# Layer-norm tiles turned back two steps behind, mixed features emitted in the next head, and four early output tiles stored, in a one-core mLSTM and HGRN2 step

## The chip, the cores and the metric

The kernel runs on one NeuronCore of one Trainium2 chip. The metric is the time of one execution on the device in microseconds. The core has a matrix engine (TensorE, PE in the profile, with its weight loads under PEld), a vector engine (VectorE, DVE), an activation engine (ScalarE, ACT), GpSimd (POOL), and SyncE (SP), which here only issues transfers. PE writes into PSUM; the kernel divides it into three pools of banks of 128 x 512 numbers: `mm` (three banks, projections and output tiles), `lv` (two) and `o` (three).

## What is computed

One layer of a decoder trunk over a prompt of 1024 tokens and eight samples of eight new tokens (64 rows, "tile 8" of nine 128-row tiles, in the kernel's words; the other eight tiles are the prompt). Everything is float32. The model width is 1024; four mLSTM heads with keys of 128 and values of 256, eight HGRN2 heads of 128.

```python
xn = rmsnorm(x, g_norm)
xm, zm, om, fh, qh, ih, zh = split(xn @ w_in)
xc = silu(causal_conv(xm)); q, k from xc, v from xm, per head; gates from [q, k, v]
# mLSTM, per chunk: C is the matrix memory, n its normaliser, m a running maximum
num = (q k^T * D) v + g * (q C);  den = rowsum(q k^T * D) + g * (q n)
h   = num / max(|den|, exp(-m));  C = decay * C + sum_s w_s k_s v_s^T
hm = layernorm(h, m_ln) * sigmoid(om)
hm = (hm + m_skip * xc) * silu(zm)             # the "mixed" features of the mLSTM heads
# HGRN2, per chunk: S = diag(f) S + k v^T, o = S^T q, k = 1 - f
oh = rmsnorm(o, h_norm) * silu(zh)
y = rmsnorm(x + concat(hm, oh) @ w_out, g_final)
```

The outputs are y for prompt and samples and the new states (conv rows, C, n, m and S).

## The kernel before

Float32 products are made of float32r parts: a number is split into a high and a low part, and `mm3` issues three matmuls (lines 94, 95, 96: high x high, low x high, high x low). The high part is a cast on ACT (for the input weights `whi`, line 147), the low part a subtraction on POOL (`wlo`, line 147) or DVE.

After a front (norms, conv, q, k, v of all mLSTM heads), the main part runs twelve heads in the order H0 M0 H1 M1 H2 M2 H3 M3 H4 H5 H6 H7, H an HGRN2 head (`hgrn_main`) and M an mLSTM head (`mlstm_main`). Each of these functions is a generator: it emits a piece of a head and yields a weight. `weave` takes that weight times a ratio and emits as many microseconds of side work between the pieces. The side work is the input projection of the heads to come, 48 pieces per head of weights times activations, and, at the end, the first output tiles (`early_out`). The order on PE is the order of this text (`tc.manual_schedule`); on the other engines and on the transfer queue the scheduler sets it, out of its own estimate of when each instruction is ready. A head's pieces all carry weights that sum to about `HEAD`, so that its 48 side pieces end with it.

An M head goes through eight prompt tiles j. Each is one step: PE makes the state update `pu`, the numerator `pn` (lines 94 to 96 on `o`), DVE folds C, and `layer_norm` makes the normalised tile `hn` (DVE line 657, with POOL and DVE small work ahead). `turn_back` transposes `hn` on PE (line 719) into an `lv` bank, and `onto_om` multiplies a pair of tiles onto the output gate `om` on DVE. Before, step j turns back tile j-1. Then the sample tile follows the same way (line 811), the eight sample states are updated on DVE (line 825), and last the mixed features are made for each half of the head: a load `xcr` of the conv output (line 835), `xcr * skip + om` on DVE (line 837), `* zm` on POOL (line 839), and a store to `mixd` in HBM (line 840).

An H head does its product over levels 1, 2, 4, ... 64 of the time axis. DVE makes Q and K (line 973, 937) for level 1, then `products(n)` folds gates and makes QK (lines 1005, 940, with `Sf` and `f` in 1008, 1010); PE multiplies them in groups (line 101), level 1 first, levels 2 to 8 as a group ("lower"), later 16 to 64 ("upper"). z is its gate path (line 880, on DVE from a projection in an `mm` bank).

At the end the output projection multiplies the 16 mixed features by `w_out`, in two halves of 512 columns. `wo_split` splits its weights, low halves alternately on DVE and POOL for the first half. `out_part(hf, t, g)` accumulates the first 15 features of tile t in an `mm` bank, `out_done` adds the 16th. The first five tiles (`EARLY`) are side work of the last H head; two of them are stored into `xr` (`out_store`, DVE line 1317) so that their banks are free, three stay in the three banks. Features of an output tile come back from HBM through `mraw`, with `mhi` and `mlo` on ACT and DVE (1266, 1267).

Of the kernel before, what the change touches and what calls it, by code (L numbers as in the profile page):

```python
# [30 lines left out]
def hybrid_step(  # L31
# [509 lines left out]
    def gate_scan():  # L541

        ig, y, lf, t1, m, b = [unit(s)[0:4, :T] for s in ("ig", "gy", "glf", "gt", "gm", "gb")]
        nc.sync.dma_start(out=gd, in_=GT)
        gv = gd.rearrange("(j r) t -> r j t", r=32)
        for g, dst in ((0, ig), (1, y)):
            nc.sync.dma_start(out=dst.rearrange("p (j t) -> p j t", t=272), in_=gv[4 * g:4 * g + 4])
            V.tensor_scalar(dst, dst, scalar1=bgt[:, g:g + 1], scalar2=None, op0=ALU.add)
        yield 1.0
        S.activation(t1, y, AF.Abs)  # L550
        S.activation(t1, t1, AF.Exp, scale=-1.0)
        S.activation(t1, t1, AF.Ln, bias=1.0)
        V.scalar_tensor_tensor(lf, y, 0.0, t1, op0=ALU.min, op1=ALU.subtract)
        lfs = lf[:, TP:T].rearrange("p (b c) -> p b c", c=8)[:, :, 0]
        igs = ig[:, TP:T].rearrange("p (b c) -> p b c", c=8)[:, :, 0]
        lm = small(8, "lm")
        V.tensor_tensor(lm[0:4, :], lfs, m0t, op=ALU.add)
        V.tensor_copy(t1, lf)
        V.memset(t1[:, TP:T].rearrange("p (b c) -> p b c", c=8)[:, :, 0], -1e30)
        V.tensor_copy(y, ig)  # L560
        V.tensor_tensor(y[:, TP:T].rearrange("p (b c) -> p b c", c=8)[:, :, 0], igs, lm[0:4, :], op=ALU.max)
        V.tensor_tensor_scan(m, t1, y, initial=0.0, op0=ALU.add, op1=ALU.max)
        yield 4.0
        G.memset(t1, 1.0)
# [12 lines left out]
        nc.sync.dma_start(out=o_sm[0].rearrange("b h -> h b"), in_=msl[0:4, :])
        yield 4.0
        ps = ps_o()
        for t in range(8):  # L580
            PE.transpose(ps[:, t * 8:t * 8 + 4], ig[:, t * P:t * P + P], ident[0:4, 0:4])
            PE.transpose(ps[:, t * 8 + 4:t * 8 + 8], m[:, t * P:t * P + P], ident[0:4, 0:4])
        for j in range(4):
            for o, src in ((64, ig), (68, m)):
                PE.matmul(ps[32 * j:32 * j + 32, o:o + 4], lhsT=src[:, TP + win(j):TP + win(j) + 32],
                          rhs=ident[0:4, 0:4], start=True, stop=True)
        V.tensor_copy(COLS.rearrange("p a b -> p (a b)"), ps[:, :72])
        S.activation(COLS[:, :, 4:8], COLS[:, :, 4:8], AF.Exp, scale=-2.0)
# [56 lines left out]
    def layer_norm(ps, t, h):  # L645
# [11 lines left out]
        V.tensor_scalar(hn, ps[:, 0:256], scalar1=mv[:, 0:1], scalar2=dd, op0=ALU.subtract, op1=ALU.mult)  # L657
        return hn

    def mlstm_main(h):  # L660
        d = ctxs.pop(("M", h))
        mln, msk = par("m_ln"), par("m_skip")
# [65 lines left out]
        yield 2.4  # L728
        tiles += pair_prep(1)
        yield 2.4  # L730
        C = tp = hn = None
        for j in range(8):
            Sv, kv, qv, vv = tiles[j]
            pu = ps_o()
# [11 lines left out]
            if j < 7:  # L746
# [1 line left out]
                Cs = (CC[:, o:o + VW], CC[:, o + VW:o + 2 * VW])  # L748
                S.copy(Cs[0], C)
                V.tensor_tensor(Cs[1], C, f32(Cs[0]), op=ALU.subtract)  # L750
            if j > 0:
                if j % 2:
                    tp = ps_lv()
                turn_back(hn, tp, (j - 1) % 2)
                if j % 2 == 0:
                    onto_om(tp, j // 2 - 1)
            hn = layer_norm(pn, j, h)
            if j % 2 and j < 5:
                tiles += pair_prep(j // 2 + 2)
                yield 2.4  # L760
            yield 2.8 if j else 4.2
        turn_back(hn, tp, 1)
        onto_om(tp, 3)
        nc.sync.dma_start(out=o_pC[0, 0, h], in_=C[:, 0:256])
        G.tensor_copy(NEW[:, h:h + 1], C[:, 256:257])

# [21 lines left out]
        for a in range(4):  # L788
# [5 lines left out]
        V.tensor_tensor(qm.rearrange("p (b c) -> p b c", c=72)[:, :, 0:8], q[:, TP:T].rearrange("p (b c) -> p b c", c=8),  # L794
                        Gt[:, TP:T].rearrange("p (b c) -> p b c", c=8), op=ALU.mult)
        yield 5.0
        pn = ps_o()
        for j in range(4):
            oj = pn[32 * j:32 * j + 32, :257]
# [5 lines left out]
                PE.matmul(oj, lhsT=qm[:, b * 64 + win(j):b * 64 + win(j) + 32], rhs=C0v[b // 4][:, b % 4, :],  # L805
                          start=False, stop=e == 1)
        hn = layer_norm(pn, 8, h)
        yield 3.0
        tp = ps_lv()
        for a in range(2):  # L810
            PE.transpose(tp[:, a * P:(a + 1) * P], hn[:, a * P:(a + 1) * P], ident)
        for a in range(2):
            oms, ts = compact(d["om"][a][:, TP:T]), spread(tp[:, a * P:(a + 1) * P])
            for e in range(2):
                V.scalar_tensor_tensor(oms[:, e], ts[:, e], mln[:, 2 * h + a:2 * h + a + 1], oms[:, e],
                                       op0=ALU.mult, op1=ALU.mult)
        for a in range(4):
            for g in range(2):
                pu = ps_o()
# [4 lines left out]
                cv = C0v[g][:, a, :]  # L824
                new = V.scalar_tensor_tensor(cv, cv, Gt[:, TP + 8 * b + 7:TP + 8 * b + 8], pu[:, :257],
                                             op0=ALU.mult, op1=ALU.add)
            yield 1.3
        NEWv = NEW[:, 4:36].rearrange("p (b h) -> p h b", h=4)
        for i in range(2):
            nc.sync.dma_start(out=o_sC[0, 4 * i:4 * i + 4, h].rearrange("b k v -> k b v"), in_=C0v[i][:, :, 0:256])  # L830
            G.tensor_copy(NEWv[:, h, 4 * i:4 * i + 4], C0v[i][:, :, 256])
        for a in range(2):
            ft = 2 * h + a
            xc = unit("xcr")
            nc.sync.dma_start(out=xc[:, :T], in_=xcd[ft])
            with tc.issue_after(getattr(new, "ins", new)):
                V.scalar_tensor_tensor(xc[:, :T], xc[:, :T], msk[:, ft:ft + 1], d["om"][a][:, :T],
                                       op0=ALU.mult, op1=ALU.add)
            G.tensor_tensor(xc[:, :T], xc[:, :T], d["zm"][a][:, :T], op=ALU.mult)
            nc.sync.dma_start(out=mixd[ft], in_=xc[:, :T])  # L840
            yield 1.8

    def norm_states():
        pt = ps_o()
# [72 lines left out]
    def hgrn_main(h):  # L917
# [316 lines left out]
    def wo_split(hf, i):  # L1234
        raw = wo_raw.pop((hf, i))
        if hf == 0 or i >= 6:
            hi, lo = XH[:, i * 1024:(i + 1) * 1024], XL[:, i * 1024:(i + 1) * 1024]
        else:
            hi, lo = unit("woh", F32R)[:, :1024], unit("wol", F32R)[:, :1024]
        S.copy(hi, raw)  # L1240
        (G if hf == 0 and i % 2 else V).tensor_tensor(lo, raw, f32(hi), op=ALU.subtract)
        for a in range(2):
            wo[(hf, 2 * i + a)] = (hi[:, a * 512:(a + 1) * 512], lo[:, a * 512:(a + 1) * 512])

# [35 lines left out]
    def out_part(hf, t, g):  # L1280
# [4 lines left out]
        ps = acc[(hf, t)]  # L1285
        mx = ctxs.pop("mix0") if (hf, t, g) == (0, 0, 0) else mix_prep(t, g)
        for k in range(len(mx)):
            stop = (hf, t, g, k) in ((0, 0, 1, 6), (0, 1, 1, 6))
            mm_out(ps, t, mx[k], wo[(hf, g * 8 + k)], g == 0 and k == 0, stop)
            if k % 2 or k + 1 == len(mx):  # L1290
                yield cost(6, 512)
# [6 lines left out]

    def out_store(t):

        if t == 0:
            part[1] = unit("xr")
        part[t] = part[1][:, t * HU:(t + 1) * HU]
        x_res(part[t], 0, t)
        V.tensor_tensor(part[t][:, :512], part[t][:, :512], acc.pop((0, t)), op=ALU.add)

# [42 lines left out]
            yield from g  # L1349

    STEPS = 48
    HEAD = {"H": 47.2, "M": 53.4}

    def weave(side, main, ratio):

# [14 lines left out]
                yield from islice(gates, 1)  # L1370
        yield from gates

    EARLY = 5

    def early_out():
        for t in range(EARLY):
            for g in range(2):
# [1 line left out]
                    for i in range(4 + 2 * g, 6 + 2 * g):  # L1379
                        wo_prep(0, i)  # L1380
                yield from out_part(0, t, g)
            if t < EARLY - 3:
                out_store(t)

    side = chain(*[(hgrn_in if kind == "H" else mlstm_in)(h) for kind, h in jobs], early_out())
# [18 lines left out]
    with tc.manual_schedule(engines={mybir.EngineType.PE}):  # L1404
        for i, (kind, h) in enumerate(jobs[:-1]):
            main = (hgrn_main if kind == "H" else mlstm_main)(h)
            extra = 0.0
            if i == 0:
                main, extra = with_gates(main, gates), 9.0
            weave(islice(side, STEPS), main, us / (HEAD[kind] + extra))  # L1410
        weave(side, hgrn_main(7), (us / 2 + EARLY * cost(45, 512)) / HEAD["H"])
        for t in range(9):
            out_done(0, t)
            if EARLY - 3 <= t < 6:
                run(chain(out_part(0, t + 3, 0), out_part(0, t + 3, 1)))
# [97 lines left out]
```

## Time and profile before

| | |
|---|---|
| median of 3 runs | 1219.85 us (1218.01 to 1223.15) |
| profiled execution | 1220.89 us, span of its instructions 1219.1 us |
| granted PE clock, mean | 0.983 |
| PE busy | 1139.4 us, 93% |
| DVE busy | 771.5 us, 63% |
| ACT busy | 437.4 us, 36% |
| POOL busy | 389.3 us, 32% |

A row of waits reads: engine, what waited, `<-` what released it, then the total in us, the times and the longest. A row of a timeline reads: start, length, engine, line, operation, output `<-` inputs, shape, how many in a row, and in brackets the engine's idle time just ahead with what ended it. A stretch reads: from, to, length, the engine's busy time with its instructions, the granted clock as a share of full speed, the share and the GB/s of the transfers.

### The profile page before, as it was taken

The page shows a single profiled execution, that of the slowest core. Times are in us where ns is not written, and L with a number is a line of the kernel's source. Part 1 is how long each engine was busy: PE and PEld are TensorE (multiplying, and loading weights), DVE is VectorE, ACT ScalarE, POOL GpSimd, SP SyncE. Part 2 cuts the span into 40 slices and gives each one's busy share as a digit, 9 for nine tenths or more (in the row PEclk, how much of TensorE's full clock was granted, in tenths as well). Part 3 has the DMA queues.
Part 4 walks back from the last instruction along what each step waited for, and adds up shares of the span by engine and source line. Part 5 has one row for each costly group of instructions (what it writes and reads, how often), then busy time and mean ns, then how long its engine had stood idle before and what let it go on. Part 6 is the DMA issues. An engine that isn't in the chain of part 4 may idle for free. (4 is left out here: it accounts for less than half of the span.)

```text
span 1219.1 us, 22869 instructions
## 1 busy us (share of the span) xinstructions
PE 1139.4 (93%) x9251; PEld 1064.6 (87%) x9251; DVE 771.5 (63%) x1474; ACT 437.4 (36%) x937; POOL 389.3 (32%) x508
## 2 busy tenths in 40 slices
PE   6899999979988999899998999899999989989997
PEld 5789999979988998899988998899999978767886
DVE  4674544595669466875669466876868686533443
ACT  5454444425321443134321453142424233333332
POOL 4443333223434343523434352533232331100000
PEclk9899999999999999999999999999999999989999
DMA  8133334123133232414132331412121245556652
GB/s 262 45 129 134 129 122 135 35 54 125 60 115 107 84 114 74 148 53 146 34 120 98 110 106 57 143 54 73 53 74 53 73 143 141 166 157 180 210 175 99
DMA packets 154061, 133.89 MB, mean 110 GB/s; under 512 B 11439, under 2 KB 130155, under 8 KB 153954
## 3 DMA queue, kind: packets, MB, share of 16 engines
q1 hardware_dynamic: 153954, 132.41, 34.6%
q8 instruction: 73, 1.20, 0.4%
q14 instruction: 34, 0.28, 0.1%
HBM read 93.96 MB, written 38.43 MB: 109 GB/s over the span
## 5 line engine op out<-in xcount | busy, mean ns | idle before, releaser
L94 PE MATMUL mm<-XH,whi 128*128 128x384 f32 (+1 forms) x1344 | 454.3, 338 | 0.9 <-DVE z L880 0.6
L95 PE MATMUL mm<-XL,whi 128*128 128x384 f32 (+1 forms) x1344 | 442.6, 329 | 0.0
L96 PE MATMUL mm<-XH,wlo 128*128 128x384 f32 (+1 forms) x1344 | 442.1, 329 | 0.0
L94 PEld LDWEIGHTS mm<-XH,whi 128*128 128x128 f32 x1344 | 255.7, 190 | 5.7 <-issue 1.7
L95 PEld LDWEIGHTS mm<-XL,whi 128*128 128x128 f32 x1344 | 255.9, 190 | 1.7 <-issue 1.3
L96 PEld LDWEIGHTS mm<-XH,wlo 128*128 128x128 f32 x1344 | 255.0, 190 | 0.0
L147 POOL TENSOR_TENSOR wlo<-wraw,whi 128x1024 fp32r<-128x1024 f32 x56 | 139.5, 2491 | 226.5 <-ACT whi L147 226.0
L147 ACT CAST whi<-wraw 128x1024 fp32r<-128x1024 f32 x56 | 58.9, 1051 | 123.4 <-PE mm L95 104.5
L94 PE MATMUL mm<-XH,mhi 128*128 128x512 f32 x144 | 59.2, 411 | 10.1 <-ACT lv L1322 4.6
L96 PE MATMUL mm<-XH,mlo 128*128 128x512 f32 x144 | 57.8, 401 | 1.2 <-DVE mlo L1267 1.2
L1266 ACT CAST mhi<-mraw 128x1024 fp32r<-128x1024 f32 (+1 forms) x32 | 31.9, 998 | 74.7 <-PE mm L95 56.2
L95 PE MATMUL mm<-XL,mhi 128*128 128x512 f32 x144 | 57.7, 401 | 0.0
L1335 POOL TENSOR_TENSOR rs<-rs,mhalf 128x1 f32<-128x1 f32 (+1 forms) x9 | 4.9, 542 | 158.3 <-DVE rs L1334 158.3
L1267 DVE TENSOR_TENSOR mlo<-mraw,mhi 128x1024 fp32r<-128x1024 f32 (+1 forms) x32 | 39.0, 1221 | 24.0 <-ACT mhi L1266 23.8
L940 DVE TENSOR_TENSOR QK<-hk,Sf 128x256 f32<-128x256 f32 x96 | 49.4, 555 | 0.0
L457 DVE TENSOR_TENSOR xml<-mm,xmh 128x384 fp32r<-128x384 f32 (+1 forms) x24 | 12.1, 508 | 52.2 <-ACT XB L456 45.0
L872 DVE TENSOR_SCALAR f<-f,OML,LB 128x384 f32<-128x384 f32 (+1 forms) x24 | 26.8, 1116 | 27.2 <-ACT f L870 27.1
L94 PEld LDWEIGHTS mm<-XH,mhi 128*128 128x128 f32 x144 | 27.9, 194 | 17.2 <-issue 5.0
L1008 DVE TENSOR_TENSOR Sf<-Sf,f 128x512 f32<-128x512 f32 (+1 forms) x48 | 40.1, 836 | 0.1
L892 ACT COPY iT<-mm 128x128 f32<-128x128 f32 x64 | 13.0, 270 | 73.3 <-PE mm L96 70.3
L473 DVE SCALAR_TENSOR_TENSOR Y<-XB,PAR,Y 128x1112 f32<-128x1112 f32 x24 | 38.1, 1589 | 0.2
L96 PE MATMUL mm<-woh,mlo 128*128 128x512 f32 x96 | 37.5, 391 | 0.3 <-DVE mlo L1267 0.3
(350 smaller groups left out, 2237.0 us busy)
## 6 DMA issues: line engine op xcount, KB each, us to landing
wraw<-in_w_in SPq DMA_DIRECT2D x56, 512.0 KB, 4.2
woraw<-in_w_out SPq DMA_DIRECT2D x16, 512.0 KB, 4.4
mraw<-mixd SPq DMA_DIRECT2D x16, 512.0 KB, 6.2
mraw<-mixd SPq DMA_DIRECT2D x16, 448.0 KB, 4.5
xcd<-XB SPq DMA_DIRECT2D x8, 544.0 KB, 2.7
qkd<-qk SPq DMA_DIRECT2D x16, 272.0 KB, 5.0
xcr<-xcd SPq DMA_DIRECT2D x8, 544.0 KB
mixd<-xcr SPq DMA_DIRECT2D x8, 544.0 KB
```

The source lines that it names most:

```text
L94: PE.matmul(out, lhsT=lh, rhs=rh, start=first, stop=False)
L95: PE.matmul(out, lhsT=lh, rhs=rl, start=False, stop=False)
L96: PE.matmul(out, lhsT=ll, rhs=rh, start=False, stop=last)
L147: return S.copy(hi, raw), G.tensor_tensor(lo, raw, f32(hi), op=ALU.subtract)
L457: V.tensor_tensor(ml[:, t0:t0 + m], ps[:, :m], f32(mh[:, t0:t0 + m]), op=ALU.subtract)
L473: V.scalar_tensor_tensor(Y[:, :1112], XB[:, j:j + 1112], cw[:, 8 * j + ft:8 * j + ft + 1], Y[:, :1112], op0=ALU.mult, op1=ALU.add)
L872: V.tensor_scalar(f[:, s], f[:, s], scalar1=OML[:, h:h + 1], scalar2=LB[:, h:h + 1], op0=ALU.mult, op1=ALU.add)
L892: S.copy(dst, ps[:, u * P:(u + 1) * P])
L940: i = V.tensor_tensor(dst, ksrc, ssrc, op=ALU.mult)
L1008: V.tensor_tensor(hv(Sf, W, n)[:, :, 0, :], hv(Sf, W, n)[:, :, 0, :], hv(f, W, n)[:, :, 1, n - 1:n].to_broadcast([P, ng, n]), op=ALU.mult)
L1266: S.copy(hi[:, :w * n], raw[:, :w * n])
L1267: V.tensor_tensor(lo[:, :w * n], raw[:, :w * n], f32(hi[:, :w * n]), op=ALU.subtract)
```

## The change

There are five parts.

1. `gate_scan`, woven into the first H head, yields 5.5 in place of 4.0, twice, and that head's weight grows from 9 to 12 on top.
2. The turn-back in an M head goes two steps behind (`hns` holds the tiles waiting), the last tile's after the 5.0 yield, the sample tile's in the second of the four state updates. Weights are changed (4.2 to 2.8, 3.0 to 2.0, 1.3 to 1.5, `HEAD["M"]` from 53.4 to 48.2).
3. The mixed features are put off (`deferred`) into the H head that follows, behind `products(2)` and `products(4)`; that head's weight grows by 3.6.
4. `wo_split` makes all low halves on DVE.
5. Four of the five early tiles are stored (`STORED`), two to a unit; out_part runs in the out_done loop from t = 3 to 6, for tile t+2, in place of t = 2 to 5, tile t+3.

```diff
-        yield 4.0
+        yield 5.5          # gate_scan, twice
...
+            if j > 1:
+                if j % 2 == 0:
+                    tp = ps_lv()
+                turn_back(hns.pop(0), tp, j % 2)
                 if j % 2:
-                    tp = ps_lv()
-                turn_back(hn, tp, (j - 1) % 2)
-                if j % 2 == 0:
                     onto_om(tp, j // 2 - 1)
-            hn = layer_norm(pn, j, h)
+            hns.append(layer_norm(pn, j, h))
...
-            yield 2.8 if j else 4.2
-        turn_back(hn, tp, 1)
-        onto_om(tp, 3)
+            yield 2.8
+        tp = ps_lv()
+        turn_back(hns.pop(0), tp, 0)
...
         yield 5.0
+        turn_back(hns.pop(0), tp, 1)
+        onto_om(tp, 3)
...
         hn = layer_norm(pn, 8, h)
-        yield 3.0
-        tp = ps_lv()
-        ...                # tile 8: transposes and products onto om
+        yield 2.0
         for a in range(4):
             ...            # two state updates
-            yield 1.3
+            if a == 1:
+                ...        # tile 8: transposes and products onto om
+            yield 1.5
...
-        for a in range(2):
+        def mixed(a):
             ft = 2 * h + a
             xc = unit("xcr")
             nc.sync.dma_start(out=xc[:, :T], in_=xcd[ft])
-            with tc.issue_after(getattr(new, "ins", new)):
-                V.scalar_tensor_tensor(...)
+            V.scalar_tensor_tensor(...)
             G.tensor_tensor(xc[:, :T], xc[:, :T], d["zm"][a][:, :T], op=ALU.mult)
             nc.sync.dma_start(out=mixd[ft], in_=xc[:, :T])
-            yield 1.8
+        deferred.extend([lambda: mixed(0), lambda: mixed(1)])
...
+        late = [deferred.pop(0) for _ in range(len(deferred))]      # hgrn_main
...
         for n in (2, 4, 8):
             lower.append(products(n))
+            if late:
+                with tc.issue_after(getattr(lower[-1][3], "ins", lower[-1][3])):
+                    late.pop(0)()
+                yield 1.8
             yield 3.3
...
-        (G if hf == 0 and i % 2 else V).tensor_tensor(lo, raw, f32(hi), op=ALU.subtract)
+        V.tensor_tensor(lo, raw, f32(hi), op=ALU.subtract)
...
-            stop = (hf, t, g, k) in ((0, 0, 1, 6), (0, 1, 1, 6))
+            stop = hf == 0 and t < STORED and (g, k) == (1, 6)
...
-    HEAD = {"H": 47.2, "M": 53.4}
+    HEAD = {"H": 47.2, "M": 48.2}
...
-    EARLY = 5
+    EARLY, STORED = 5, 4
...
-            if t < EARLY - 3:
+            if t < STORED:
                 out_store(t)
...
+            if kind == "H" and i and jobs[i - 1][0] == "M":
+                extra = 3.6
             if i == 0:
-                main, extra = with_gates(main, gates), 9.0
+                main, extra = with_gates(main, gates), 12.0
...
-            if EARLY - 3 <= t < 6:
-                run(chain(out_part(0, t + 3, 0), out_part(0, t + 3, 1)))
+            if 3 <= t < 7:
+                run(chain(out_part(0, t + 2, 0), out_part(0, t + 2, 1)))
```

PE issues the same 6141 rows in both. Line numbers of the changed kernel are a few higher (719 is 721 there, 837 is 843, 839 is 845, 940 is 947, 1005 is 1013, 1318 is 1330).

On PE, in the third M head (M2), the end of the step of tile 7: the numerator `o_...` of tile 7 is made, then a turn-back of `hn_...` into `lv_...`, then side work on `mm`. Before, the turn-back is of tile 6:

```order
L94 MATMUL o_6752<-vhl_6540,skl_6554 128x258
L95 MATMUL o_6752<-vhl_6540,skl_6554 128x258
L96 MATMUL o_6752<-vhl_6540,skl_6554 128x258
L94 MATMUL o_6752<-CC_6254,qgl_6544 128x258
L95 MATMUL o_6752<-CC_6254,qgl_6544 128x258
L96 MATMUL o_6752<-CC_6254,qgl_6544 128x258
L719 MATMUL lv_6761<-CF,hn_6727 128x128 x2
L94 MATMUL mm_6729<-XH,whi_6435 128x384
```

Now:

```order
L94 MATMUL o_6758<-vhl_6543,skl_6557 128x258
L95 MATMUL o_6758<-vhl_6543,skl_6557 128x258
L96 MATMUL o_6758<-vhl_6543,skl_6557 128x258
L94 MATMUL o_6758<-CC_6262,qgl_6547 128x258
L95 MATMUL o_6758<-CC_6262,qgl_6547 128x258
L96 MATMUL o_6758<-CC_6262,qgl_6547 128x258
L721 MATMUL lv_6724<-CF,hn_6684 128x128 x2
L94 MATMUL mm_6782<-XH,whi_6432 128x320
```

In its place now stands the turn-back of tile 5 (`hn_6684`); tile 6 is turned after the loop, eighteen side products later, and twelve side products and nine products of a tile lie between one turn-back and the next at this place.

On DVE, from the last sample state of the last M head into the H head behind it (M3 to H4). `xcr` is the mixed features, `hq` the last two q blocks, Q and K what PE needs for level 1. Before:

```order
L825 SCALAR_TENSOR_TENSOR C_1175_8339<-C_1175_8339,RB_7750,o_8514 128x257
L837 SCALAR_TENSOR_TENSOR xcr_8529<-xcr_8529,PAR,om_7353 128x1088
L880 TENSOR_TENSOR hq_8172<-hq_8172,mm_8467 128x384
L837 SCALAR_TENSOR_TENSOR xcr_8546<-xcr_8546,PAR,om_7580 128x1088
L880 TENSOR_TENSOR hq_8172<-hq_8172,mm_8518 128x320
L973 TENSOR_TENSOR Q_1209_8564<-hq_8172,f_8170 128x544
L937 COPY K_1210_8567<-hk_8171 128x256
L937 COPY K_1210_8567<-hk_8171 128x4x64
L988 COPY Sf_8563<-f_8170 128x544
L990 TENSOR_TENSOR f_8170<-f_8170 128x544
```

Now, in the same H head, the stretch behind the level-2 products, `QK_8655`, up to the level-4 products, `QK_8701`:

```order
L947 TENSOR_TENSOR QK_8655<-hk_8167,Sf_8553 128x4x32x2
L949 TENSOR_TENSOR QK_8655<-hk_8167,Sf_8553 128x64
L843 SCALAR_TENSOR_TENSOR xcr_8662<-xcr_8662,PAR,om_7347 128x1088
L971 COPY_PREDICATED A_1205_8551<-mk_364,lv_8606 128x288
L1016 TENSOR_TENSOR Sf_8553<-Sf_8553,f_8166 128x272x2
L974 COPY_PREDICATED A_1205_8551<-mk_365,lv_8606 128x144
L1018 TENSOR_TENSOR f_8166<-f_8166 128x272x2
L947 TENSOR_TENSOR QK_8701<-hk_8167,Sf_8553 128x64x4
L947 TENSOR_TENSOR QK_8701<-hk_8167,Sf_8553 128x4x16x4
L949 TENSOR_TENSOR QK_8701<-hk_8167,Sf_8553 128x64
L1013 TENSOR_TENSOR QK_8701<-hq_8168,f_8166 128x544
L1016 TENSOR_TENSOR Sf_8553<-Sf_8553,f_8166 128x136x4
```

The first `xcr` row has moved from ahead of Q and K to behind the level-2 products; the second stands two rows further down, ahead of the level-8 products. On PE, 90 side products now lie between the level-1 group and the lower group there, before 78; between the last sample-state product and the level-1 group there are 36, before 54.

On SP at the same place, the loads and stores (`wraw` a block of input weights, `out<-C` the sample states). Before:

```order
L140 DMA wraw_8722<-in_w_in 128x8x128
L835 DMA xcr_8529<-xcd 128x1088
L835 DMA xcr_8546<-xcd 128x1088
L830 DMA out<-C_1174_8338 128x4x256
L830 DMA out<-C_1175_8339 128x4x256
L840 DMA mixd<-xcr_8529 128x1088
L840 DMA mixd<-xcr_8546 128x1088
L140 DMA wraw_8904<-in_w_in 128x8x128
```

Now:

```order
L836 DMA out<-C_1174_8346 128x4x256
L836 DMA out<-C_1175_8347 128x4x256
L140 DMA wraw_8898<-in_w_in 128x8x128
L842 DMA xcr_8662<-xcd 128x1088
L842 DMA xcr_8708<-xcd 128x1088
L846 DMA mixd<-xcr_8662 128x1088
```

The `xcr` loads stood ahead of the state stores; now they stand behind them and behind the next weight load.

On DVE, at the output tiles, from the last rows of the last H head (z, `zl`, `zh`) to the adds onto `xr`. `wol` is a low half of the second half's output weights, `mlo` that of an output tile's features. Before:

```order
L1216 SCALAR_TENSOR_TENSOR z_10391<-lv_11661,PAR,z_10391 128x32 x2
L1146 TENSOR_TENSOR zl_11448<-z_10391,zh_11447 128x512
L1241 TENSOR_TENSOR wol_11780<-woraw_11777,woh_11779 128x1024
L1146 TENSOR_TENSOR zh_11447<-z_10391,zh_11447 128x64
L1318 TENSOR_TENSOR xr_11207<-xr_11207,o_11682 128x512
L1267 TENSOR_TENSOR mlo_11753<-mraw_11750,mhi_11752 128x896
L1318 TENSOR_TENSOR xr_11207<-xr_11207,o_11696 128x512
L1318 TENSOR_TENSOR xr_11710<-xr_11710,mm_11314 128x512
```

Now:

```order
L1253 TENSOR_TENSOR wol_11726<-woraw_11723,woh_11725 128x1024
L1279 TENSOR_TENSOR mlo_11741<-mraw_11738,mhi_11740 128x1024
L1228 SCALAR_TENSOR_TENSOR z_10391<-lv_11666,PAR,z_10391 128x32 x2
L1158 TENSOR_TENSOR zl_11448<-z_10391,zh_11447 128x512
L1158 TENSOR_TENSOR zh_11447<-z_10391,zh_11447 128x64
L1330 TENSOR_TENSOR xr_11207<-xr_11207,o_11687 128x512
L1279 TENSOR_TENSOR mlo_11771<-mraw_11768,mhi_11770 128x896
L1330 TENSOR_TENSOR xr_11207<-xr_11207,o_11701 128x512
L1330 TENSOR_TENSOR xr_11478<-xr_11478,o_11715 128x512
L1330 TENSOR_TENSOR xr_11478<-xr_11478,o_11729 128x512
```

The `wol` row has moved ahead of z and the first `mlo` of the next output tile; of the adds, the first four read `o` banks now, before two, and the third read an `mm` bank.

More of the change, by code (lines that the diff above doesn't have):

```diff
@@ L577, in gate_scan @@
         nc.sync.dma_start(out=o_sm[0].rearrange("b h -> h b"), in_=msl[0:4, :])
-        yield 4.0
+        yield 5.5
         ps = ps_o()
@@ L658, in layer_norm @@
         return hn
+    deferred = []
     def mlstm_main(h):
@@ L730, in mlstm_main @@
         yield 2.4
-        C = tp = hn = None
+        C = tp = None
+        hns = []
         for j in range(8):
@@ L750, in mlstm_main @@
                 V.tensor_tensor(Cs[1], C, f32(Cs[0]), op=ALU.subtract)
-            if j > 0:
+            if j > 1:
+                if j % 2 == 0:
+                    tp = ps_lv()
+                turn_back(hns.pop(0), tp, j % 2)
                 if j % 2:
-                    tp = ps_lv()
-                turn_back(hn, tp, (j - 1) % 2)
-                if j % 2 == 0:
                     onto_om(tp, j // 2 - 1)
-            hn = layer_norm(pn, j, h)
+            hns.append(layer_norm(pn, j, h))
             if j % 2 and j < 5:
@@ L807, in mlstm_main @@
         hn = layer_norm(pn, 8, h)
-        yield 3.0
-        tp = ps_lv()
-        for a in range(2):
[L811 to L816, printed above, removed]
+        yield 2.0
         for a in range(4):
@@ L826, in mlstm_main @@
                                              op0=ALU.mult, op1=ALU.add)
-            yield 1.3
+            if a == 1:
+                tp = ps_lv()
+                for b in range(2):
+                    PE.transpose(tp[:, b * P:(b + 1) * P], hn[:, b * P:(b + 1) * P], ident)
+                for b in range(2):
+                    oms, ts = compact(d["om"][b][:, TP:T]), spread(tp[:, b * P:(b + 1) * P])
+                    for e in range(2):
+                        V.scalar_tensor_tensor(oms[:, e], ts[:, e], mln[:, 2 * h + b:2 * h + b + 1], oms[:, e],
+                                               op0=ALU.mult, op1=ALU.mult)
+            yield 1.5
         NEWv = NEW[:, 4:36].rearrange("p (b h) -> p h b", h=4)
@@ L831, in mlstm_main @@
             G.tensor_copy(NEWv[:, h, 4 * i:4 * i + 4], C0v[i][:, :, 256])
-        for a in range(2):
+        def mixed(a):
             ft = 2 * h + a
@@ L835, in mlstm_main @@
             nc.sync.dma_start(out=xc[:, :T], in_=xcd[ft])
-            with tc.issue_after(getattr(new, "ins", new)):
-                V.scalar_tensor_tensor(xc[:, :T], xc[:, :T], msk[:, ft:ft + 1], d["om"][a][:, :T],
-                                       op0=ALU.mult, op1=ALU.add)
+            V.scalar_tensor_tensor(xc[:, :T], xc[:, :T], msk[:, ft:ft + 1], d["om"][a][:, :T],
+                                   op0=ALU.mult, op1=ALU.add)
             G.tensor_tensor(xc[:, :T], xc[:, :T], d["zm"][a][:, :T], op=ALU.mult)
             nc.sync.dma_start(out=mixd[ft], in_=xc[:, :T])
-            yield 1.8
+        deferred.extend([lambda: mixed(0), lambda: mixed(1)])
     def norm_states():
@@ L1299, in out_store @@
     def out_store(t):
-        if t == 0:
-            part[1] = unit("xr")
-        part[t] = part[1][:, t * HU:(t + 1) * HU]
+        if t % 2 == 0:
+            ctxs["xr"] = unit("xr")
+        part[t] = ctxs["xr"][:, t % 2 * HU:(t % 2 + 1) * HU]
         x_res(part[t], 0, t)
```

## The prediction

> **What bounds the kernel now.** I read the page's first part, then what PE waited for, then the timelines around the longest waits.
>
> ```profile
> span 1219.1 us, 22869 instructions
> PE 1139.4 (93%) x9251; PEld 1064.6 (87%) x9251; DVE 771.5 (63%) x1474; ACT 437.4 (36%) x937; POOL 389.3 (32%) x508
> PE lv L719 <- DVE hn L657: 15.3, 16, 1.6
> PE lv L101 <- DVE K L937: 13.3, 4, 3.3
> PE mm L94 <- ACT lv L1322: 4.6, 1, 4.6
> PE lv L101 <- DVE QK L1005: 4.6, 2, 2.8
> PE mm L94 <- DVE z L880: 4.3, 3, 3.7
> PE lv L811 <- DVE hn L657: 2.7, 4, 0.7
> PE lv L1108 <- ACT A L1055: 1.8, 1, 1.8
> PE mm L94 <- DVE xr L1318: 1.7, 2, 0.9
> PE mm L1276 <- DVE xr L1318: 1.1, 1, 1.1
> ```
>
> PE is the bound, busy 93%. Its instructions are the same in number in both kernels, so only its waits (total us, times, longest) and the clock can change. The change touches: the layer-norm waits L719 and L811 (18.0 us), the first products of an H head behind an M head (L101 on K, 13.3), one wait on z (3.7), and at the output tiles 4.6 + 1.7 + 1.1.
>
> Some waits cost more than their length, as stretches of PE's record show (length, PE busy, granted clock, then DMA):
>
> ```profile
> 787.59:791.00 3.41, 3.41 (x13) 0.50 0.19 54
> 995.81:999.22 3.41, 3.41 (x10) 0.50 0.89 269
> 1067.49:1074.32 6.83, 4.97 (x12) 0.50 0.84 265
> 268.77:272.18 3.41, 3.41 (x13) 0.50 0.56 138
> ```
>
> The first begins 1.6 us after the 3.34 us wait for K, the second 0.7 us after the wait on z, the third inside the 4.6 us wait, the fourth after the 2.8 us wait on QK. Half a clock for 3.41 us loses 1.7 us of work; the third loses 4.97 / 2 = 2.5.
>
> **Layer norms.** Turning each tile back one step later puts another step ahead of the turn-back: nine products of 258 columns and at least twelve side products. A side product is 0.17 us apart here:
>
> ```profile
> 862.34 0.33 PE L95 MATMUL mm<-XL,whi 128*128 128x384 f32 x1
> 862.51 0.33 PE L96 MATMUL mm<-XH,wlo 128*128 128x384 f32 x1
> 863.30 0.49 PE L101 MATMUL lv<-QK 128*32 128x32 f32 x34
> ```
>
> Twelve are 2.0 us, above the longest L719 wait, 1.6; so all 18.0 can go. The bounds are 0 and 18.0. I take 16: where a step gets thinner (4.2 to 2.8 at the first tile) the state C, which DVE folds for the next tile, may come late instead, a few tenths a time.
>
> **From an M head to the next H head.** Before, DVE's and POOL's mixed features stand between the last q block and K:
>
> ```profile
> 774.51 1.35 DVE L837 SCALAR_TENSOR_TENSOR xcr<-xcr,PAR,om 128x1088 f32<-128x1088 f32 x1
> 776.24 3.40 DVE L837 SCALAR_TENSOR_TENSOR xcr<-xcr,PAR,om 128x1088 f32<-128x1088 f32 x1
> 782.75 3.11 DVE L937 COPY K<-hk 128x256 f32<-128x256 f32 x2
> 775.94 2.55 POOL L839 TENSOR_TENSOR xcr<-xcr,zm 128x1088 f32<-128x1088 f32 x1
> 786.01 0.65 PE L101 MATMUL lv<-Q,K 128*32 128x64 f32 x32 [3.34 <-DVE K L937]
> ```
>
> The second L837 took 3.40 instead of 1.35 while POOL's product ran: a DVE operation on SBUF operands that meets a large POOL one waits about 2.1 us. Without the mixed features there, the place looks like one H head behind another, where PE has no such wait:
>
> ```profile
> 843.61 0.31 PE L96 MATMUL mm<-XH,wlo 128*128 128x320 f32 x1
> 844.93 2.41 POOL L147 TENSOR_TENSOR wlo<-wraw,whi 128x1024 fp32r<-128x1024 f32 x1 [6.82 <-ACT whi L147]
> 849.18 0.61 PE L101 MATMUL lv<-Q,K 128*32 128x64 f32 x29
> 857.21 0.76 DVE L940 TENSOR_TENSOR QK<-hk,Sf 128x256 f32<-128x256 f32 x2
> 857.88 0.69 DVE L1005 TENSOR_TENSOR QK<-hq,f 128x512 f32<-128x512 f32 x1
> 858.48 2.90 DVE L1008 TENSOR_TENSOR Sf<-Sf,f 128x512 f32<-128x512 f32 x1
> 858.16 2.66 POOL L147 TENSOR_TENSOR wlo<-wraw,whi 128x1024 fp32r<-128x1024 f32 x1 [8.28 <-ACT whi L147]
> ```
>
> So 13.3 us go, and four half-clock stretches, 4 x 1.7 = 6.8: 20.1 together (between 13.3 and 20.1).
>
> What is late next? Here q's last product gives way to the next at 843.75 (call it T; its row starts at 843.61), PE's first group starts at T + 5.4, DVE's operands for the second group (863.30, T + 19.55) are ready at 858.5, T + 14.8. The change puts two L837 into exactly this stretch, 2 x 1.35 = 2.7: T + 17.5. Each is followed by its POOL product, and the next DVE operations read SBUF only: 2 x 2.1, T + 21.7. POOL's next wlo (L147) stands right behind the second product and can stop a third: T + 23.8. PE's way is longer too: 90 side products lie between the two groups instead of 78, 12 x 0.174 = 2.1 on top of T + 19.55, so it arrives at T + 21.6. The new wait is 0 with one stop, 0.1 with two, 2.2 with three. I take three, since wlo is queued with nothing between: 4 x 2.2 = 8.8. The 1.8 us waits (L1108, and the first of the two on QK) had no half clock behind them, the 2.8 us one had. The new 2.2 lies between, so I add four tenths of 6.8, 2.7: back 11.5 (bounds 0 and 4 x (2.2 + 1.7) = 15.6). The net of the boundaries is 20.1 - 11.5 = 8.6.
>
> [...]
>
> On SP's queue the two xcr loads now stand behind two state stores and the next weight load. The first multiply is wanted about T + 8.6. The weight load goes out as soon as POOL's wlo has freed a buffer, at 844.93 + 2.41 = T + 3.6, and a weight load lands in 4.2 us; an xcr load just behind it at T + 8 to 8.5. It is in time with nothing to spare. I take 0 and keep 1.5 us a head for the range.
>
> ```profile
> wraw<-in_w_in SPq DMA_DIRECT2D x56, 512.0 KB, 4.2
> 785.06 14.55 SPq L140 DMA_DIRECT2D wraw<-in_w_in  x2
> ```
>
> **The weights' low halves on DVE** (wo_split): four POOL operations become four DVE ones of 1.23. The wait on z belongs here:
>
> ```profile
> 984.88 5.19 POOL L1241 TENSOR_TENSOR XL<-woraw,XH 128x1024 fp32r<-128x1024 f32 x2 [7.50 <-DMA woraw<-in_w_out]
> 985.18 5.19 DVE L940 TENSOR_TENSOR QK<-hk,Sf 128x256 f32<-128x256 f32 x2
> 994.51 0.54 DVE L880 TENSOR_TENSOR z<-z,mm 128x384 f32<-128x384 f32 x1
> 995.11 0.51 PE L94 MATMUL mm<-XH,mhi 128*128 128x512 f32 x1 [3.68 <-DVE z L880]
> ```
>
> Two L940 took 5.19 beside POOL's two; the pair at 857.21 takes 0.76. That is 4.4 saved against 2 x 1.23 = 2.5 of new DVE work ahead of z, and the weight loads, whose buffers POOL gave back, start sooner. The wait and its half clock are 3.7 + 1.7 = 5.4; I take 4.5 off (bounds 0 and 5.4).
>
> **Four stored tiles.** Before the output's third tile PE waits for a bank that DVE's add frees late:
>
> ```profile
> 1065.05 1.23 DVE L1241 TENSOR_TENSOR wol<-woraw,woh 128x1024 fp32r<-128x1024 f32 x1 [4.22 <-ACT woh L1240]
> 1066.33 0.68 DVE L1318 TENSOR_TENSOR xr<-xr,o 128x512 f32<-128x512 f32 x1
> 1068.53 0.68 DVE L1318 TENSOR_TENSOR xr<-xr,mm 128x512 f32<-128x512 f32 x1
> 1069.35 0.76 PE L94 MATMUL mm<-XH,mhi 128*128 128x512 f32 x1 [4.64 <-ACT lv L1322]
> ```
>
> With four tiles out of their banks the next tile has a free one. But four short products now run through three o banks, and the fourth waits for the first add (1066.33 + 0.68 = 1067.0 by this trace, against PE free at 1064.7): 2.3 at worst, less since the weight load now stands ahead of the features' loads. I leave 1 of 4.64 + 2.5 = 7.1, gain 6 (bounds 1 and 7.1), and of the bank waits 1.7 + 1.1 I take 2. Two more adds of 0.68 in the last head lie under PE's work.
>
> **Gates.** The heavier first-head weights move about 0.8 us of side work; the QK waits there are DVE's chain, so I take 0 (bounds -1 and +2).
>
> **Sum.** 16 + 8.6 + 4.5 + 6 + 2 = 37.1. The profiled execution took 1220.89, 1.0 above the median of 1219.85: 1220.9 - 37.1 - 1.0 = 1182.8, with about 1 us for small new waits in the re-weighed heads 1184. All terms at their bounds in favour, no new wait: 18.0 + 20.1 + 5.4 + 7.1 + 2.8 = 53.4, 1166.
>
> **Rivals.**
> A: the second group pays in full. The xcr loads land 1.5 us late and every gap draws a half clock: 4 x (2.2 + 1.5 + 1.7) = 21.6 instead of 11.5, time 1194. For it: the loads have nothing to spare. Against: 1.8 us gaps kept the clock.
> B: wlo comes later than the second product (it came 8.3 us after POOL's last work in the H-to-H rows); two stops, no new wait: 11.5 less, 1172.
> C: the tail gives nothing since its weight loads still land late: 12.5 more, 1196. Against: the bank is free whatever they do.
> D, slower: the xcr loads stall SP's queue. They sit behind a weight load that is held until a buffer is free, as the 14.55 us pair of issues shows. A load late by x costs 4 x x on top of the full gaps 4 x 3.9: it decides once 4 x (x + 3.9) passes the other gains, 16 + 20.1 + 12.5 = 48.6, at x = 8.3. At 11 us, 1230. Against: this buffer's user, wlo, ends before K.
> E: the turn-backs' moved waits come back as waits on C and the time at the layer norms stays: 16 more, 1200.
>
> **How the numbers follow.** Forecast 0.42, A 0.2, B 0.16, C 0.08, E 0.06, D 0.04, nothing moves 0.04. The time is the forecast's, 1184. The range runs from 1170 (B and 2 us of the favourable bounds) to 1206 (A with C). About 0.5%, 6 us, can be told from no change: faster 0.91, same 0.04, slower 0.05.
>
> **What would show it.** Right: no row of PE waiting for hn; no wait on K at the four boundaries and full clock there; a short wait of L101 on QK some 14 us later; the 4.6 and 3.7 us waits gone. Wrong: PE waits on xcr-delayed QK of over 4 us, POOL's xcr and wlo not back to back, or waits on C inside M heads.

## The result, and the profile after

The changed kernel takes 1193.62 us (1192.67 to 1193.89), against 1220.7 before on the same chip: 0.9777 of it, 95% interval 0.9755 to 0.980. That is 27.1 us less; the prediction's sum was 37.1 and its time 1184. One execution of e1 (2236.95 us, the profiled one, so that e1 has no trace to compare) and one of e4 (1845.89 us) were slow, and the medians given for these two are of their other three executions (with the slow one e4's would be 1173.69, the 1173.7 that a later expectation uses). The page and PE's waits of the changed kernel (engine, what waited, what released it, total us, times, longest):

```profile
span 1191.8 us, 22884 instructions
PE 1135.1 (95%) x9251; PEld 1065.4 (89%) x9251; DVE 783.5 (66%) x1480; ACT 438.7 (37%) x937; POOL 380.7 (32%) x504
PE lv L1120 <- ACT A L1063: 13.8, 5, 4.1
PE lv L101 <- DVE QK L947: 8.7, 4, 3.1
PE mm L96 <- DVE mlo L1279: 2.4, 4, 0.8
PE mm L94 <- DVE z L887: 2.1, 1, 2.1
PE lv L101 <- DVE K L944: 1.1, 1, 1.1
```

The waits on hn, on K at the four places and all waits on banks at the output are gone. Two rows are new or grown. The 8.7 us on QK is the wait that the prediction put at 8.8. The 13.8 us of L1120 on A is one that it did not have; before, the same wait (L1108 there) was 1.8 us, once. Of the 13.8, 4.1 fall in the first H head and 9.7 in the four H heads behind an M head.

The way to the second group in the last of these (M3 to H4), in DVE's, POOL's and PE's timelines:

```profile
771.31 1.35 DVE L843 SCALAR_TENSOR_TENSOR xcr<-xcr,PAR,om 128x1088 f32<-128x1088 f32 x1 [1.45 <-DMA xcr<-xcd]
772.94 2.93 DVE L1016 TENSOR_TENSOR Sf<-Sf,f 128x544 f32<-128x544 f32 x1
779.56 1.34 DVE L843 SCALAR_TENSOR_TENSOR xcr<-xcr,PAR,om 128x1088 f32<-128x1088 f32 x1
781.42 5.22 DVE L947 TENSOR_TENSOR QK<-hk,Sf 128x256 f32<-128x256 f32 x2
772.74 2.55 POOL L845 TENSOR_TENSOR xcr<-xcr,zm 128x1088 f32<-128x1088 f32 x1 [5.50 <-DVE xcr L843]
780.98 2.91 POOL L845 TENSOR_TENSOR xcr<-xcr,zm 128x1088 f32<-128x1088 f32 x1 [5.70 <-DVE xcr L843]
783.85 2.52 POOL L147 TENSOR_TENSOR wlo<-wraw,whi 128x1024 fp32r<-128x1024 f32 x1
786.70 0.46 PE L101 MATMUL lv<-QK 128*32 128x32 f32 x32 [3.08 <-DVE QK L947]
```

There are the three stops: 2.93 where 0.71 is usual (778.17 in the same head), and 5.22 for a pair that takes 0.76, first beside POOL's second product and then beside wlo with nothing between. Here the load of xcr is also 1.45 us late, and the wait is 3.08; at the other three places it is 1.84 to 1.96. The first load was late at three of the four places, by 0.87, 0.16 and 1.45 us; in DVE's waits of the whole run that is one row:

```profile
DVE xcr L843 <- DMA xcr<-xcd: 2.5, 3, 1.4
```

In the third of the four heads (M2 to H3) wlo came ahead of the second product and not right behind it. The stops were three there too: 2.92, 2.94 and 3.06 us.

Then the same head twenty microseconds on, on DVE, ACT and PE:

```profile
796.96 2.78 DVE L1018 TENSOR_TENSOR f<-f 128x512 f32<-128x512 f32 x1
803.11 0.28 DVE L1100 TENSOR_TENSOR Vs<-V,Vs 128x128 fp32r<-128x128 f32 x1
803.41 0.29 DVE L974 COPY_PREDICATED A<-mk,lv 128x128 f32<-128x128 uint8 x1
803.43 1.28 ACT L1104 ACTIVATE VL<-Vs,CF 128x128 fp32r<-128x128 f32 x4 [4.61 <-DVE Vs L1100]
804.61 1.80 ACT L1063 COPY A<-lv 32x128 f32<-32x128 f32 x6
806.47 1.11 PE L1120 MATMUL lv<-CF,iT 128*128 128x128 f32 x4 [3.21 <-ACT A L1063]
```

DVE is still late, and one more wlo stops it (2.78, where 0.69 is usual, as at 787.75). ACT stands 4.61 us at the cast VL because DVE's Vs is late. Its copies of A, the release of the `lv` bank, stand behind VL on ACT. PE's transposes need that bank and wait 3.21. In the kernel before, the same two ACT groups ran without such a stop, and the A copies waited 0.38 us, for DVE's mask:

```profile
816.12 1.27 ACT L1092 ACTIVATE VL<-Vs,CF 128x128 fp32r<-128x128 f32 x4
817.76 1.82 ACT L1055 COPY A<-lv 32x128 f32<-32x128 f32 x6 [0.38 <-DVE A L967]
```

Stretches of PE in the changed kernel (from and to, length, busy, granted clock, then transfers):

```profile
541.30:545.30 4.00, 4.00 (x32) 1.00 0.02 4
786.70:790.70 4.00, 4.00 (x57) 1.00 0.47 135
392.61:396.02 3.41, 3.41 (x15) 0.50 0.48 135
672.50:675.91 3.41, 3.41 (x16) 0.50 0.00 0
805.62:812.45 6.83, 5.98 (x25) 0.50 0.00 0
276.56:283.39 6.83, 6.83 (x51) 0.50 0.17 50
```

The half clock did not go with the waits. The first two rows begin at the end of gaps of 2.70 and 3.08 us and have the full clock; the third follows a gap of 1.96 and has half. So the length of a gap does not tell. In that third stretch products of 128x320 follow each other every 0.267 us (ten from 393.17 to 395.84), at the full clock every 0.146 (nine from 542.20 to 543.51).

The trace does show what tells. All half-clock stretches of the main part begin whole multiples of 3.413 us apart (276.56 to 392.61 is 34 of them, on to 672.50 is 82, on to 805.62 is 39: 529.06 us in 155 steps). Cut on this grid, these are the windows just ahead of the last three, at 389.20, 669.09 and 802.21, and the windows that hold the larger part of the two gaps without half clock:

```profile
389.20:392.61 3.41, 1.45 (x67) 1.00 0.51 187
539.38:542.79 3.41, 1.49 (x12) 1.00 0.11 27
669.09:672.50 3.41, 0.74 (x7) 1.00 0.47 128
785.14:788.55 3.41, 1.85 (x43) 1.00 0.51 178
802.21:805.62 3.41, 0.88 (x6) 1.00 0.62 167
```

PE is idle for 1.96, 2.67 and 2.53 us of the windows that half clock follows, and for 1.92 and 1.56 of the other two: the gaps of 2.70 and 3.08 us were split over two windows. I cut eleven traces this way (before, changed, e2 to e10; from 240 to 1140 us; windows that themselves had full clock). All 48 windows with 1.96 us or more of idle time were followed by half clock, and none with 1.82 or less was; of the seven between, four were. Ahead of 240 us, where the front runs other shapes, less was enough (1.50 us at 37.62). The grid's place against the kernel's start differs from trace to trace (2.53 us behind it before, 0.08 now), so where a gap of 2 to 3 us falls is luck.

### The profile page after: what moved, and what is told of

The parts are those of the page before. It is cut to its first block, busy times and chain, and to the rows that moved or that the text cites. A ratio compares the mean times of both kernels' runs of the same rounds, so it can differ in the third digit from the quotient of the medians.

```text
span 1191.8 us, 22884 instructions
## 1 busy us (share of the span) xinstructions
PE 1135.1 (95%) x9251; PEld 1065.4 (89%) x9251; DVE 783.5 (66%) x1480; ACT 438.7 (37%) x937; POOL 380.7 (32%) x504
## 4 chain that ended last, share of the span: by engine, by line
PE 53%; DVE 13%; DMA 6%; ACT 2%; issue 2%; POOL 1%; SPq 0%; POOLq 0%; ACTq 0%; DVEq 0%
PE mm L94 14%; PE mm L96 14%; PE mm L95 13%; DVE QK L947 3%; DVE Sf L1016 2%; DVE f L1018 2%; DMA xcr<-xcd 2%; DMA mraw<-mixd 1%; DMA woraw<-in_w_out 1%; PE o L1166 1%; DVE QK L1013 1%; DMA RB<-rd 1%; PE o L94 1%; PE o L95 1%; PE o L96 1%
## 5 line engine op out<-in xcount | busy, mean ns | idle before, releaser
L947 DVE TENSOR_TENSOR QK<-hk,Sf 128x256 f32<-128x256 f32 x96 | 54.0, 603 | 0.0
L1016 DVE TENSOR_TENSOR Sf<-Sf,f 128x512 f32<-128x512 f32 (+1 forms) x48 | 46.5, 970 | 0.1
L879 DVE TENSOR_SCALAR f<-f,OML,LB 128x384 f32<-128x384 f32 (+1 forms) x24 | 31.1, 1297 | 22.1 <-ACT f L877 22.1
L1018 DVE TENSOR_TENSOR f<-f 128x512 f32<-128x512 f32 (+1 forms) x48 | 42.2, 878 | 0.8
L1057 POOL COPY A<-A 32x32 f32<-32x32 f32 x16 | 14.7, 921 | 86.1 <-DVE A L974 85.6
```

Source lines behind the costliest of these rows:

```text
L879: V.tensor_scalar(f[:, s], f[:, s], scalar1=OML[:, h:h + 1], scalar2=LB[:, h:h + 1], op0=ALU.mult, op1=ALU.add)
L947: i = V.tensor_tensor(dst, ksrc, ssrc, op=ALU.mult)
L1016: V.tensor_tensor(hv(Sf, W, n)[:, :, 0, :], hv(Sf, W, n)[:, :, 0, :], hv(f, W, n)[:, :, 1, n - 1:n].to_broadcast([P, ng, n]), op=ALU.mult)
L1018: V.tensor_tensor(hv(f, W, n)[:, :, 1, :], hv(f, W, n)[:, :, 1, :], hv(f, W, n)[:, :, 0, n - 1:n].to_broadcast([P, ng, n]), op=ALU.mult)
L1057: G.tensor_copy(A[64 * g:64 * g + 32, TP + 32 * g:TP + 32 * g + 32], A32[64 * g:64 * g + 32, 256:288])
```

## The experiments

My theory after the result: the turn-backs and the tail gave what was forecast or more; the moved mixed features gave nothing, because DVE's lateness reached a second place, through ACT's order. The rival: the re-weighed pieces, not the move, made the new waits. All ratios are to the kernel before on the same chip, with 95% intervals. The differences from the changed kernel are of medians from different chips, on which the kernel before took 1220.7 to 1222.05; by the ratios e2 gains 12 us instead of 10.6.

**e1: the turn-backs alone.** The kernel before with part 2.

```diff
 # the changed kernel, with parts 1, 3, 4 and 5 undone
-    HEAD = {"H": 47.2, "M": 48.2}
+    HEAD = {"H": 47.2, "M": 51.8}      # mixed features stay in the M head, 2 x 1.8
```

> The kernel before with the turn-backs two steps behind and their weights, nothing else of the change. Theory: the 18.0 us of PE waiting for hn go and nothing comes back, and the 20 turn-backs themselves run shorter (3.9 us less PE time on them in the changed kernel), so 18 to 22 us less than before, 1199 to 1203. Rival: part of what the turn-backs cost comes back as waits inside the M heads on the folded state C, or as a longer wait for K (3.3 us each before): less than 15 us gained, over 1206.

Measured 1194.69 us, 0.9777 (0.9761 to 0.9793): 27 us gained, above the 18 to 22. This one part gives as much as the whole change. The rival falls.

**e2: the mixed features put back.** The changed kernel without part 3.

```diff
-        deferred.extend([lambda: mixed(0), lambda: mixed(1)])
+        for a in range(2):
+            mixed(a, new)           # issued behind the last state fold, as before
+            yield 1.8
...
-    HEAD = {"H": 47.2, "M": 48.2}
+    HEAD = {"H": 47.2, "M": 51.8}
...
-                extra = 3.6
+                extra = 0.0
```

> The changed kernel with the mixed features put back at the end of the M head. Theory: the move took away 13.3 us of waits for K and brought 8.7 us on QK and 9.7 us on A (L1120 behind H heads that follow an M head), with about as much half clock, so without it the kernel is some 4 to 6 us faster than the changed one, 1187 to 1190, with four waits for K of 3.3 us. Rival: the waits on A come from something else (the re-weighed pieces), and without the move the waits for K come on top: 1198 or more.

Measured 1183.05 us, 0.9678 (0.9663 to 0.9694): 10.6 us faster than the changed kernel, more than expected. So the move of the mixed features made the kernel slower. PE's waits in the whole run, and where K is made:

```profile
PE lv L101 <- DVE K L947: 9.4, 5, 2.1
PE lv L1123 <- ACT A L1066: 4.1, 1, 4.1
749.69 2.61 DVE L844 SCALAR_TENSOR_TENSOR xcr<-xcr,PAR,om 128x1088 f32<-128x1088 f32 x2
```

The A waits behind M heads are gone, only the first head's 4.1 is left. The K waits at the four places are 2.1 each, 8.3 together, not the 13.3 of before. Here PE has 60 side products between the last state product and the level-1 group, before 54, and DVE runs both multiplies together in 2.61, before 1.35 and 3.40. These 5.0 us (13.3 - 8.3) are about what e1 found above its forecast: 18.0 + 3.9 (e1's expectation) + 5.0 = 26.9. That is inferred from e2's rows; it was not seen in e1 itself. e2 also takes back the weights that went with the move, so alone it does not separate the rival; e4 and e5 keep them.

**e3: VL behind the copies of A.**

```diff
-            S.activation(VL[:, c], f32(Vs[:, P:2 * P]), AF.Copy, scale=vmask[:, a:a + 1])
...
-        level_run(upper)
+        cps = level_run(upper)            # the last copy of A
+        with tc.issue_after(getattr(cps, "ins", cps)):
+            for a in range(4):
+                S.activation(VL[:, ...], f32(Vs[:, P:2 * P]), AF.Copy, scale=vmask[:, a:a + 1])
```

> The changed kernel with ACT's four VL casts (L1104) placed behind its copies of A (L1063) in each H head. Theory: ACT stands at VL until DVE's late Vs (L1100), and the copies of A that PE's transposes L1120 wait for stand behind it; with the order turned the 13.8 us of L1120 waits shrink below 4 us and their half clock goes too, 1193.6 - 10 to - 14, 1180 to 1184. Rival: A is late because the upper level itself or its bank is late; then the waits stay at 12 us or more and the time at 1192 to 1195.

Measured 1184.19 us, 0.9696 (0.9672 to 0.9719), 9.4 us faster than the changed kernel. PE's waits, and ACT in M3 to H4:

```profile
PE lv L1125 <- ACT A L1064: 6.6, 5, 3.2
800.86 1.82 ACT L1064 COPY A<-lv 32x128 f32<-32x128 f32 x6 [4.90 <-DVE A L974]
802.71 1.28 ACT L1117 ACTIVATE VL<-Vs,CF 128x128 fp32r<-128x128 f32 x4
```

The waits fell from 13.8 to 6.6, behind M heads from 9.7 to 3.3; I had expected under 4 in all. Half of the theory holds. The order on ACT is a cause: turned, it takes away 6.4 of the 9.7 us. What is left has its cause one step back: the copies now stand for DVE's mask on A (L974), itself in DVE's late queue.

**e4: the mixed features behind the upper level.**

```diff
-            if late:                      # behind products(2), products(4)
-                with tc.issue_after(...): late.pop(0)()
-                yield 1.8
...
         level_run(upper)
+        for _ in range(len(late)):
+            with tc.issue_after(getattr(qmc, "ins", qmc)):      # the last DVE work ahead of it
+                late.pop(0)()
+            yield 1.8
```

> The changed kernel with the mixed features put off further, behind the upper level group of the H head, where DVE stood idle for 3.3 us twice. Theory: DVE's way to the lower group is that of an H head behind an H head again, so the 8.7 us on QK go, DVE reaches Vs earlier so that the 9.7 us on A go too, and the half clock behind them: 1193.6 - 18 to - 24, 1170 to 1176. Rival: the same 2 x 1.35 us and two stops fall on the state folds (L1176) and on the next head's gates instead, and PE waits there: less than 10 us gained, 1184 or more.

Measured 1171.8 us, 0.9591 (0.9556 to 0.9626), 22 us faster than the changed kernel, as expected. Between 300 and 800 us PE waits for only two things:

```profile
PE o L1185 <- DVE KS L1128: 2.2, 1, 2.2
PE o L1216 <- DVE osq L1138: 2.0, 2, 1.7
```

The K, QK and A waits are all gone there. The place was wrong, not the idea to move them. The heads' weights are those of the changed kernel, so the re-weighing did not make these waits: the rival falls.

**e5: the product on DVE.**

```diff
-            G.tensor_tensor(xc[:, :T], xc[:, :T], d["zm"][a][:, :T], op=ALU.mult)
+            V.tensor_tensor(xc[:, :T], xc[:, :T], d["zm"][a][:, :T], op=ALU.mult)
```

> The changed kernel with the mixed features' product (L845) on DVE instead of POOL. Theory: a DVE operation on SBUF operands that meets a large POOL operation stands still for about 2.1 us, and three such stops make the wait for QK. Two stops go (4.2) and two DVE operations of 1.35 come (2.7), so DVE is 1.5 us earlier at the lower group: the waits on QK fall from 8.7 to 2 to 4 us, those on A (L1120) by as much, 1180 to 1187. Rival: the stops are something else (the order on DVE, late loads); then DVE is 2.7 us later at each of four places, and the time 1200 or more.

Measured 1185.95 us, 0.9705 (0.9685 to 0.9726), 7.7 us faster than the changed kernel with 2.6 us more DVE work in each of the four heads. No QK row is left among PE's waits (expected 2 to 4 us); L1120 has grown a little:

```profile
PE lv L1120 <- ACT A L1063: 15.5, 5, 4.1
```

So POOL's products did stop DVE, and the stops, not DVE's own work, made the QK wait. That the A waits did not fall with it was not expected: in M3 to H4, counted from PE's level-1 group, DVE's Vs came 3.4 us earlier (33.2 us, in the changed kernel 36.6) and PE reached L1120 as much earlier (33.3, there 36.7), so the wait there stayed 3.21. DVE was met by a wlo at both of its later stops (2.81 and 2.78 us). The rows of both kernels show such stops: before, an L837 took 1.35 alone and 3.40 beside POOL's 2.55; changed, an L1016 took 0.71 alone and 2.93 beside POOL's 2.55. Not every row beside POOL grew: before, the eight of L724 (`om<-lv`, an input in PSUM) that ran beside a wlo took 0.47 to 0.48, as did the other 24.

**e6 and e9: the tail.** e6 puts the low halves of the output weights back alternately on POOL and DVE; e9 puts the two stored tiles back as well.

```diff
-        V.tensor_tensor(lo, raw, f32(hi), op=ALU.subtract)
+        (G if hf == 0 and i % 2 else V).tensor_tensor(lo, raw, f32(hi), op=ALU.subtract)     # e6 and e9
...
-    EARLY, STORED = 5, 4
+    EARLY, STORED = 5, 2        # e9 alone, with out_part at t = 2 to 5 for tile t+3
```

> The changed kernel with the low halves of the first output weights alternately on POOL and DVE again. Theory (the step on wo_split): the wait on z in the last H head and its half clock come back, 3 to 6 us, 1196 to 1200. Rival: the wait on z went because of the other parts (four stored tiles, earlier loads): 1192 to 1195.

> The changed kernel with the tail as before: low halves of the weights alternately on POOL and DVE, two stored tiles. Theory: with the low halves alone put back it took 1196.3; the four stored tiles took away 4.6 + 1.7 + 1.1 us of waits for banks and the half clock at them, so 5 to 9 us more, 1201 to 1206. Rival: the waits for banks are replaced by late loads of the features anyway, 1196 to 1199.

e6: 1196.29 us, 0.9793 (0.9771 to 0.9816); the median is 2.7 us above the changed kernel's, but the intervals of the two ratios overlap, so the time alone does not settle it. The wait does: z is 5.4 us in two waits, with 2.1 of it in the first H head as in the changed kernel. e9: 1206.95 us, 0.988 (0.9863 to 0.9897), some 13 us above the changed kernel. The waits on z of e6 and on banks of e9:

```profile
PE mm L94 <- DVE z L887: 5.4, 2, 3.3
PE mm L94 <- ACT lv L1334: 4.9, 1, 4.9
PE mm L94 <- DVE xr L1330: 1.7, 2, 0.9
PE mm L1288 <- DVE xr L1330: 1.1, 1, 1.1
```

**e7: the gate pieces' weights as before** (5.5 to 4.0 twice, 12.0 to 9.0).

> The changed kernel with the gate pieces' weights as before (4.0, 4.0, 9.0). Theory: DVE's chain sets the first H head, the waits of 7.3 us there only change their place (QK instead of K, z and A), 1191 to 1197. Rival: the heavier weights are what put 0.8 us of work ahead and spared waits: 1198 or more; or they made the wait on A of 4.1 us and the 6.8 us half clock behind it: 1190 or less.

Measured 1190.45 us, 0.9751 (0.9723 to 0.9779), 3.2 us less than the changed kernel by the medians; the intervals overlap slightly. The waits of the first H head are QK 4.3 and A 1.7, 6.0 in place of 7.3, and its half clock stretches add to 6.8 us in place of 10.2. I had taken this part for neutral; the sign points to a small loss.

**e8 and e10: towards a faster kernel.** e8 is e4 with the second half of the mixed features put behind the state folds (L1176) and e3's order on ACT; e10 is e8 with e7's weights.

```diff
         nc.sync.dma_start(out=o_pS[0, 0, h], in_=states[7])
+        if late:
+            with tc.issue_after(getattr(st_last, "ins", st_last)):
+                late.pop(0)()
+            yield 1.8
```

> The kernel with the mixed features behind the upper level group, with the second half put behind the state folds (L1176), and ACT's VL casts behind the copies of A in every H head. Theory: in the first such kernel (1173.7) the pair of POOL products still stopped DVE ahead of KS and the norm (2.2 and 1.7 us waits, one half clock); apart they hide, 1167 to 1172. Rival: the second half now delays the norm of every such head: 1174 or more.

> The kernel of 1170.6 (mixed features behind the upper level, the halves apart, VL behind the copies of A) with the gate pieces' weights as before the change. Theory: the gate weights alone cost 3 us in the changed kernel (1190.5 without them), through the wait on A of 3 to 4 us and its long half clock, so 1166 to 1169. Rival: that gain was half-clock luck; no difference, 1170 to 1172.

e8: 1170.6 us, 0.9577 (0.9546 to 0.9609). e10: 1168.44 us, 0.9566 (0.955 to 0.9582). e10 is 52 us under the kernel before and about 25 under the changed one; its step over e8 is not resolved by the intervals. From 230 us on PE waits in e10 mostly for

```profile
PE lv L101 <- DVE QK L1013: 4.6, 2, 2.8
PE o L1225 <- DVE osq L1143: 3.4, 3, 1.3
PE mm L96 <- DVE mlo L1288: 3.0, 4, 1.0
PE lv L1125 <- ACT A L1064: 1.8, 1, 1.8
```

## Why the prediction was right, and where it was off

The time, 1193.62, lies in the range 1170 to 1206 and moved the way that was said, by 27 in place of 37. By its own steps:

- **Layer norms**, taken as 16: all 18.0 us of waits went and 3.9 us of PE time on the transposes with them (time of theirs that no earlier product covered, counted in the traces: 11.8 us before, 7.9 now). The feared waits on C did not come. Mis-sized low, and by e1 and e2 the part gave some 5.0 us more, since it shortened the K waits; the prediction had no such term.
- **The boundary, what goes**: the K waits went as said. The half clock was put at 6.8 lost before and at 2.7 for what comes back, a net of 4.1. Measured, the stretches at 392.61, 672.50 and 805.62 have 3.41 + 3.41 + 5.98 = 12.8 us of PE at half clock, 6.4 lost: a net of 0.4. The 6.4 is an estimate, half of 12.8 by the granted 0.50; the spacings of 0.267 and 0.146 us would give 5.8. Of the 6.4, 1.7 follow a wait on QK, which the 2.7 was for; 4.7 follow waits on A (2.67 and 3.21 us) and belong to the next step. The term for QK was of the right size, but by luck: it took the length of the gap for the trigger, and one of the four gaps, 1.96 us, happened to fall whole into one window.
- **The boundary, what is late next**: 8.8 for QK, measured 8.7, with three stops in each head. The close agreement is in part luck. Three waits are 1.84 to 1.96, under the 2.2 forecast, and the fourth is 3.08, where the xcr load was 1.45 us late; the sum had taken that lateness as 0. And the step ended at the lower group. The upper group was not followed, nor ACT's queue, where VL stands ahead of the A copies: 9.7 us of waits and 4.7 of half clock. This is the step that failed, and the largest error. The net of the boundary, +8.6, came out as 13.3 - 8.7 - 9.7 + 0.4 = -4.7.
- **Low halves, four stored tiles**: 4.5 + 6 + 2 = 12.5 predicted; e9 gives about 13 for the two together.
- **Gates**, taken as 0: about -3 by e7, which the intervals do not resolve.

Together 21.9 - 4.7 + 13 - 3 = 27, the measured gain. So the time is in the range because the layer norms and the tail gave what was said or more; the boundary had the wrong sign. The time 1194 of rival A was close, but not for A's reason: the loads were late by 0.87, 0.16 and 1.45 us at three places, not by 1.5 at four, and one QK gap of four drew a half clock.

The half-clock stretches of the changed kernel's main part are 3.41 or 6.83 us long (3.41 at 392.61 and 672.50, 6.83 at 276.56 and 805.62) and begin whole windows of 3.413 us apart. A gap of 1.96 was followed by half clock, while one of 3.08 was not. By the traces what counts is the idle time inside one window. Why some stretches last two windows is not shown.

## What to carry to other kernels

When work is taken off one wait and put later on the same engine, follow that engine's lateness past the next consumer to every one, through the queues of other engines: here DVE was late twice, and the second time it was ACT, with the copies of A behind its VL casts, that passed it on (13.8 us of waits, 6.6 in e3 with the order turned). Here the move paid where the engine stood idle after its last urgent piece (22 us between e4 and the changed kernel), not where it was merely off the first critical wait. And a part that seems to matter only to its own waits can shrink a neighbour's: after the turn-backs the K waits that the move was to remove were worth 8.3 us, not 13.3.

## What the runs showed of the hardware

Gap length did not decide the clock: gaps of 2.70 and 3.08 us kept 1.00, one of 1.96 drew 0.50. In the main part PE's idle time within one window of a 3.413 us grid did: 1.96 us or more in a window was followed by half clock 48 times of 48, and 1.82 or less never. So a gap of 2 to 3 us can add nothing to its own length or, by an estimate (half of 3.41 us at 0.50), 1.7 us and more, by where it falls; the four K waits of 3.3 us before had 3.21, 3.01, 2.41 and 1.87 us in one window, and the last drew half clock only just.

A late transpose cost more than its wait: where 20 turn-backs waited on hn, the PE time of the transposes that no earlier product covered was 3.9 us longer as well (11.8 us, in the changed kernel 7.9).
